# Hyena filters kept as sum and difference, their channel sums as columns, and one listed order for taps, norms, spectra and projections

## The chip, the core and the metric

The kernel runs on one core of a Trainium2 chip, as one launch. The metric is device time in microseconds (us); the median of 3 runs of the kernel before is 1652.36 us (1650.11 to 1653.74). The engines are named as the profile names them: PE is TensorE, PEld its weight loads, DVE is VectorE, ACT is ScalarE, POOL is GpSimd, and SP is the queue that issues the DMAs.

## The reference, cut to what matters

Two transformer blocks on a sequence of 512 rows and a context of 256 rows, 1024 wide. Block 0 mixes with an FFT over groups and with a long convolution (Hyena), block 1 with latent attention; a gated FFN follows each. The change lies in block 0, in the filters of the long convolution:

```
h = h @ w4                                # [L, 1024]: 512 forward, 512 backward taps
h_fwd = h[:, :D_HYENA] * decay
h_bwd = h[:, D_HYENA:] * decay
two_sided = concat([h_fwd, zeros(1), h_bwd[:0:-1]])
two_sided = two_sided / sum(abs(two_sided), axis=0)
spectrum = rfft(two_sided)                # for L = 512 and for L = 256
...
u_h = dwconv3(proj[..., D_FOURIER:], conv_w, conv_b)
x0, x1, v = split(u_h, 3)
y_h = x0 * long_conv(v * x1, spectrum, hy_bias)
```

## The kernel before, in words

All products are in three passes: an operand is split into a high part in fp32r (ACT, helper `hi`, lines 119 to 124) and a low remainder (DVE, helper `lo`, line 129), and `mm3` (lines 149 to 151) adds high by high, low by high and high by low. So a weight tile takes a DMA (`wr`), an ACT copy (`wh`), a DVE subtraction (`wl`) and then the matmuls. `wr`, `wh` and `wl` have three buffers each, and the large PSUM tiles `mm` (two banks each) three, the small ones `ms` two.

`mixer` first makes the filter MLP, the norm and three projections (m = 0, 1, 2) in an order written out by hand, up to the third sine of the MLP, `h3`. What follows is the stage of the change:

- There are six time tiles of 128 taps, two (4 and 5) for the context and four (0 to 3) for the sequence. `time_tile` makes one: `filter_mm` (line 421) two fp32 matmuls of 512 columns, forward and backward; `filter_pm` multiplies each by the decay on DVE (lines 430 and 431), then POOL adds and subtracts (line 437, twice), ACT makes the high parts `aph` and `amh`, takes the absolute values (lines 441 and 442), and POOL adds those (line 443); `filter_lo` makes the low parts on DVE.
- `filter_sum` sums the absolute values over the taps: one fp32 matmul of 512 columns for each tile against a 128 by 128 matrix of a constant (line 459), so that the sum stands in all 128 rows; then a reciprocal over 128 by 512 on DVE (line 461).
- `filter_spec` makes one spectrum tile: a cosine half and a sine half, 6 matmuls each for the context (two spectra) and 12 each for the sequence (four spectra). `filter_scale` multiplies by the reciprocal on DVE (lines 497 and 499) and adds the skip row on POOL (498). `filter_nyquist` (line 475) makes one further row.
- Between them stand projections 3, 4 and 5 (`proj`, `hconv`): 48 matmuls each, and for 4 and 5 a convolution over three taps, whose first step is on ACT (line 371) and the other two on DVE (lines 372 and 373), reading PSUM. After the stage come projections 12, 8, 13, 9 and so on, each with such a convolution; `fold` (POOL, line 696, then DVE, lines 701 and 702) and the transposes of `turn` on PE (line 708) stand between them.
- `gemv_dve` (line 241) computes modulation rows on DVE from a 512 KB weight tile; 14 of them are spread over this stage and the projections after it.

The stage before is written step by step, and the scheduler of the tile layer chooses the order on each engine, but for two waits on the last step of the norm (`issue_after`). An engine works through its queue in order.

Of the kernel before, what the change touches and what calls it, by code (L numbers as in the profile page):

```python
# [18 lines left out]
P = 128  # L19
# [45 lines left out]

MIX_ORDER = """
# [10 lines left out]
class Builder:  # L77
# [118 lines left out]
    def load_sb(self):  # L196
        nc = self.nc
        for j in range(2):
            nc.sync.dma_start(self.sb[:, j, :], self.I["cboth"][j : j + 1, :].partition_broadcast(P))
            nc.scalar.activation(self.sb[:, j, :], self.sb[:, j, :], AF.Silu)  # L200

# [31 lines left out]
    def gemv_dve(self, i, jt, conds=(0, 1)):  # L233

        nc = self.nc
        raw = self.t(self.W, [P, 1024], F32, "wr")
        nc.sync.dma_start(raw, self.I["wmodT"][i, jt])
        for j in conds:
            junk = self.t(self.sbp, [P, D], BF16, "junk", 1)
            acc = self.t(self.sm, [P, 1], F32, "gacc", 4)  # L240
            nc.vector.scalar_tensor_tensor(junk, raw, 1.0, self.sb[:, j, :], op0=ALU.mult, op1=ALU.mult, accum_out=acc)  # L241
            nc.vector.tensor_tensor(self.mod[i][:, jt, j : j + 1], acc, self.col(f"bm_{i}", jt), op=ALU.add)
# [174 lines left out]
    def filter_mm(self, h3, tt):  # L417
        ps = self.mm()
        r0, c = 64 * (tt // 3), 128 * (tt % 3)
        for q in range(2):  # L420
            self.nc.tensor.matmul(ps[:, 512 * q : 512 * q + 512], h3[r0 : r0 + 64, c : c + 128], self.w4[r0 : r0 + 64, 512 * q : 512 * q + 512],
                                  start=True, stop=True)
        return ps

    def filter_pm(self, ps, dec, first):

        nc, v = self.nc, self.nc.vector
        f = self.t(self.S2, [P, 512], F32, "s2")
        b = self.t(self.S2, [P, 512], F32, "s2")
        v.tensor_tensor(f, ps[:, 0:512], dec, op=ALU.mult)  # L430
        v.tensor_tensor(b, ps[:, 512:1024], dec, op=ALU.mult)
        if first:
            v.memset(b[0:1, :], 0.0)
        parts = []
        for tg, op in (("ap", ALU.add), ("am", ALU.subtract)):
            s = self.t(self.S2, [P, 512], F32, "s2")
            nc.gpsimd.tensor_tensor(s, f, b, op=op)  # L437
            hi = self.t(self.pg, [P, 512], F32R, tg + "h", 4)
            self.hi(hi, s)
            parts.append((s, hi))  # L440
        nc.scalar.activation(f, f, AF.Abs)
        nc.scalar.activation(b, b, AF.Abs)
        nc.gpsimd.tensor_tensor(f, f, b, op=ALU.add)
        return parts, f

    def filter_lo(self, parts):
        out = []
        for tg, (s, hi) in zip(("ap", "am"), parts):
            lo = self.t(self.pg, [P, 512], F32R, tg + "l", 4)
            self.lo(lo, s, hi)  # L450
            out.append((hi, lo))
        return out

    def filter_sum(self, sums, nhalf):

        ps = self.ms()
        on = self.onesN[nhalf]
        for i, f in enumerate(sums):
            self.nc.tensor.matmul(ps, on, f, start=i == 0, stop=i == len(sums) - 1)
        S = self.t(self.pf, [P, 512], F32, "S")  # L460
        self.nc.vector.reciprocal(S, ps)
        return S

    def filter_skip(self, nhalf):
        B = self.brow
        self.nc.vector.tensor_scalar(B, B, self.bscale / nhalf, None, op0=ALU.mult)
        self.bscale = nhalf

    def filter_nyquist(self, a, S):
        v = self.nc.vector  # L470
        ps = self.ms()
        nt = len(a)
        for i in range(nt):
            for q in range(2):
                self.nc.tensor.matmul(ps[0:1, :], self.altr, a[i][0][q], start=i == 0 and q == 0, stop=i == nt - 1 and q == 1)
        ny = self.t(self.S2, [P, 512], F32, "s2")
        v.tensor_tensor(ny[0:1, :], ps[0:1, :], S[0:1, :], op=ALU.mult)
        v.tensor_tensor(ny[0:1, :], ny[0:1, :], self.brow[0:1, :], op=ALU.add)
        return ny

    def filter_spec(self, a, tb):

        nt = len(a)
        th, tl = tb
        ps = self.mm()
        for c in range(2):
            for i in range(nt):
                w = slice(256 * i + 128 * c, 256 * i + 128 * c + 128)
                self.mm3(ps[:, 512 * c : 512 * c + 512], th[:, w], tl[:, w], a[i][c][0], a[i][c][1], i == 0, i == nt - 1)
        return ps  # L490

# [1357 lines left out]
```

## Time and profile before

| | |
|---|---|
| median of 3 runs | 1652.36 us |
| profiled execution, time | 1653.27 us |
| its span | 1651.5 us |
| PE, busy share of the span | 97% |
| DVE, busy share | 64% |
| ACT, busy share | 37% |
| POOL, busy share | 8% |
| granted PE clock, mean | 0.987 |

The span runs from the first to the last instruction of the profiled execution, and all times in the trace count from its start. The profile gives for each instruction its start, its duration and, where its engine stood idle before it, what ended the idle time. Ends of matmuls are modelled, so the rate of a run of matmuls is better read from the starts of the first and of the one that follows the last.

### The profile page before, as it was taken

Reading aid. Unit: us, or ns where it says so; the run is one execution under the profiler, and the core shown is the slowest. Engines: PE = TensorE matmul, PEld = TensorE weight load, DVE = VectorE, ACT = ScalarE, POOL = GpSimd, SP = SyncE. Lnnn points to the kernel's source line nnn. Section 1 sums busy time; section 2 is a strip of 40 time slices with the busy share of each in tenths; the row PEclk is TensorE's granted clock in tenths of the full one; section 3 lists DMA queues with packets and bytes.
Section 4 is the critical chain, followed back from the end, with each engine's and each line's share of the span. In section 5 each row is a group of like instructions: output and inputs, shape, how many; then the busy total and the mean of one; then the engine's idle time right before and its main releaser. Section 6 shows DMA issues by size and latency. Waiting matters only on the chain.

```text
span 1651.5 us, 20777 instructions
## 1 busy us (share of the span) xinstructions
PE 1598.3 (97%) x8228; PEld 1298.8 (79%) x8228; DVE 1057.5 (64%) x1696; ACT 616.9 (37%) x876; POOL 125.5 (8%) x177
## 2 busy tenths in 40 slices
PE   7989998999999999999998999999999999999999
PEld 5757887888888888888887887666659878878877
DVE  6788869977877354553443576899987544344243
ACT  4432224424222112322122245989864432233131
POOL 0151115000000000000000000222210000000000
PEclk9999999999999999999999999999999999999999
DMA  9325411532444134431430420000014222222222
GB/s 360 118 77 184 173 58 62 181 136 92 154 153 152 64 128 140 145 137 64 140 115 29 147 68 20 13 10 13 1 70 162 88 101 91 89 102 91 89 90 89
DMA packets 54541, 173.35 MB, mean 105 GB/s; under 512 B 6187, under 2 KB 9453, under 8 KB 53421
## 3 DMA queue, kind: packets, MB, share of 16 engines
q1 hardware_dynamic: 54445, 172.03, 29.8%
q8 instruction: 65, 1.06, 0.3%
q14 instruction: 31, 0.25, 0.1%
HBM read 166.24 MB, written 5.77 MB: 104 GB/s over the span
## 4 chain that ended last, share of the span: by engine, by line
PE 77%; DVE 14%; issue 2%; POOL 2%; ACT 2%; DMA 2%; POOLq 0%; SPq 0%; DVEq 0%; ACTq 0%
PE mm L149 23%; PE mm L151 22%; PE mm L150 22%; PE pv L1519 2%; DVE S L1495 1%; DVE wl L129 1%; PE s L1465 1%; DVE junk L241 1%; POOL s L437 1%; DVE wr L1534 1%; PE k L149 1%; PE k L151 1%; PE k L150 1%; DVE hl L311 1%; DMA wm<-wmod0a 1%
## 5 line engine op out<-in xcount | busy, mean ns | idle before, releaser
L149 PE MATMUL mm<-hh,wh 128*128 128x512 f32 (+2 forms) x1360 | 481.9, 357 | 8.4 <-DVE x L373 6.6
L150 PE MATMUL mm<-hl,wh 128*128 128x512 f32 (+2 forms) x1360 | 479.6, 353 | 2.3 <-DVE hl L311 2.3
L151 PE MATMUL mm<-hh,wl 128*128 128x512 f32 (+2 forms) x1360 | 479.3, 353 | 1.6 <-DVE wl L129 1.6
L124 ACT ACTIVATE wh<-wr 128x1024 fp32r<-128x1024 f32 (+2 forms) x192 | 197.6, 1032 | 583.4 <-PE mm L150 545.3
L129 DVE TENSOR_TENSOR wl<-wr,wh 128x1024 fp32r<-128x1024 f32 (+2 forms) x192 | 233.8, 1220 | 253.4 <-ACT wh L124 251.7
L149 PEld LDWEIGHTS mm<-hh,wh 128*128 128x128 f32 x1360 | 256.8, 189 | 56.5 <-issue 14.6
L150 PEld LDWEIGHTS mm<-hl,wh 128*128 128x128 f32 x1360 | 257.3, 189 | 40.4 <-DVE hl L311 3.5
L151 PEld LDWEIGHTS mm<-hh,wl 128*128 128x128 f32 x1360 | 257.1, 189 | 38.4 <-DVE wl L129 1.8
L241 DVE SCALAR_TENSOR_TENSOR junk<-wr,sb 128x1024 bf16<-128x1024 f32 x128 | 157.2, 1228 | 31.6 <-DMA wr<-wmodT 31.0
L151 PE MATMUL mm<-ah,wl 128*128 128x512 f32 (+1 forms) x480 | 172.4, 359 | 0.0
L150 PE MATMUL mm<-al,wh 128*128 128x512 f32 (+1 forms) x480 | 172.2, 359 | 0.0
L149 PE MATMUL mm<-ah,wh 128*128 128x512 f32 (+1 forms) x480 | 172.1, 359 | 0.0
L1061 DVE SCALAR_TENSOR_TENSOR xr<-mm,mod,xr 128x512 f32<-128x512 f32 (+1 forms) x100 | 61.8, 632 | 152.3 <-PE mm L151 150.6
L149 PEld LDWEIGHTS mm<-ah,wh 128*128 128x128 f32 x480 | 90.3, 188 | 14.8 <-issue 0.2
L150 PEld LDWEIGHTS mm<-al,wh 128*128 128x128 f32 x480 | 90.3, 188 | 14.6
L151 PEld LDWEIGHTS mm<-ah,wl 128*128 128x128 f32 x480 | 90.2, 188 | 14.5
L1519 PE MATMUL pv<-S,V 128*128 128x512 f32 x192 | 93.8, 597 | 2.7 <-ACT S L1498 2.7
L1085 ACT ACTIVATE fg<-fg 128x772 f32<-128x772 f32 (+1 forms) x44 | 32.6, 741 | 98.4 <-DVE fg L373 98.3
L1473 ACT ACTIVATE S<-s,rks 128x512 f32<-128x512 f32 x96 | 62.6, 685 | 12.2 <-PE pv L1519 8.3
L1519 PEld LDWEIGHTS pv<-S,V 128*128 128x128 f32 x192 | 34.4, 190 | 34.9 <-issue 29.4
L1491 POOL PARTITION_ALL_REDUCE mx<-mx x16 | 45.2, 2823 | 163.1 <-DVE mx L1488 163.1
L1495 DVE TENSOR_TENSOR S<-S,mx 128x1536 f32<-128x1536 f32 x32 | 55.3, 1749 | 2.3 <-POOL mx L1491 2.3
(333 smaller groups left out, 2290.1 us busy)
## 6 DMA issues: line engine op xcount, KB each, us to landing
wr<-w_up SPq DMA_DIRECT2D x88, 512.0 KB, 3.2
wr<-wmodT SPq DMA_DIRECT2D x80, 512.0 KB, 3.2
wr<-w_dn SPq DMA_DIRECT2D x32, 512.0 KB, 3.2
wm<-wmod0a SPq DMA_DIRECT2D x8, 1024.0 KB, 9.0
wr<-w_in SPq DMA_DIRECT2D x16, 512.0 KB, 3.3
wr<-w_out SPq DMA_DIRECT2D x13, 512.0 KB, 3.3
wr<-w_dn SPq DMA_DIRECT2D x17, 384.0 KB, 3.3
wr<-w_o SPq DMA_DIRECT2D x11, 512.0 KB, 3.2
```

The costliest lines, as they stand in the source:

```text
L124: self.nc.scalar.activation(dst, src, AF.Copy)
L129: (eng or self.nc.vector).tensor_tensor(dst, src, hi.bitcast(F32), op=ALU.subtract)
L149: mmul(out, wh, xh, start=start, stop=False)
L150: mmul(out, wh, xl, start=False, stop=False)
L151: mmul(out, wl, xh, start=False, stop=stop)
L241: nc.vector.scalar_tensor_tensor(junk, raw, 1.0, self.sb[:, j, :], op0=ALU.mult, op1=ALU.mult, accum_out=acc)
L1061: nc.vector.scalar_tensor_tensor(x[m][:, a2:b2], ps[:, a2:b2], mod[:, 8 * sec + m, c : c + 1], x[m][:, a2:b2], op0=ALU.mult, op1=ALU.add)
L1085: nc.scalar.activation(g[:, :n], g[:, :n], AF.Silu)
L1473: nc.scalar.activation(c.S[a][j // 3][:, j % 3, :], c.ps[a, j], AF.Copy, scale=c.r[:, g : g + 1])
L1491: nc.gpsimd.partition_all_reduce(c.m[a][:, 1, :], c.m[a][:, 0, :], P, bass.bass_isa.ReduceOp.max)
L1495: v.tensor_tensor(c.S[a][h], c.S[a][h], mb.to_broadcast([P, 3, T]), op=ALU.subtract)
L1519: nc.tensor.matmul(c.P[a], V[:, j, o : o + 128], c.S[a][j // 3][:, j % 3, :], start=j == 0, stop=j == 5)
```

## The change

What it does, part by part:

1. `filter_w4` replaces the forward and backward columns of the weight `w4` by their sum and their difference, before the taps are made: two POOL instructions and one ACT copy, placed inside the norm, after step 0 of row block 4. The tap matmuls then give sum and difference at once, so POOL's add and subtract for each time tile go away. Row 0 of tiles 0 and 4, where the backward tap is zero, is mended by one DVE and two ACT instructions on one row (`f_row`, `f_row2`).
2. |forward| + |backward| is taken as the greater of |sum| and |difference|: one DVE instruction for each tile (`f_max`) in place of POOL's addition. The tiles are then added on POOL (`f_add`, one instruction for the context, three for the sequence).
3. The sum over the taps has the data as the stationary operand and a column of the constant as the moving one (`f_sum`, four matmuls of 1 column), so that the sums stand as 4 columns; the reciprocal is of 128 by 4 (`f_rec`); four matmuls against the identity spread it over the rows (`f_spread`), and ACT copies it (`f_scale`).
4. The whole stage, from the first tap to the last half spectrum, with projections 3, 4 and 5, the loads for projection 12 and six of the 14 `gemv_dve`, is a list of steps, `FILTER_ORDER`, and the order of PE, DVE, ACT and POOL is that of the list. The DMAs stand in the order that the scheduler gives them. Each half of a spectrum and each quarter of a projection is a step of its own.
5. Eight `gemv_dve` stay in the loop over projections 12, 8, 13 and so on, in the counts 0, 1, 1, 2, 1, 2, 1 (before: 1, 2, 1, 2, 1, 2, 2, after three in the stage).
6. The loads of the skip row and of the modulation input are issued before the stage; the Silu on the latter becomes a step of the list.

Lines in the kernel after are 9 higher than before in the helpers: `hi` is line 133, `lo` 138, and `mm3` 158 to 160.

```diff
+FILTER_ORDER = """
+D0 MM0 PMa0 MM5 Rb R4 PMb0 U0 R3 PMb5 PMa5 MM4 D3 PMb4 WH3 U2 PMa4 WH4 U1 WL3 RR0 D1 WHb SB RR4 MM2 Z0 MM3 SK1
...
-    def filter_pm(self, ps, dec, first):
...
-        v.tensor_tensor(f, ps[:, 0:512], dec, op=ALU.mult)
-        v.tensor_tensor(b, ps[:, 512:1024], dec, op=ALU.mult)
...
-            nc.gpsimd.tensor_tensor(s, f, b, op=op)
...
-        nc.scalar.activation(f, f, AF.Abs)
-        nc.scalar.activation(b, b, AF.Abs)
-        nc.gpsimd.tensor_tensor(f, f, b, op=ALU.add)
...
+    def filter_w4(self):
+
+        f, b = self.w4[:, 0:512], self.w4[:, 512:1024]
+        t = self.t(self.S2, [P, 512], F32, "s2")
+        self.nc.gpsimd.tensor_tensor(t, f, b, op=ALU.add)
+        self.nc.gpsimd.tensor_tensor(b, f, b, op=ALU.subtract)
+        self.nc.scalar.copy(f, t)
...
-            self.onesN[nh] = self.t(self.pf, [P, P], F32, f"on{int(nh)}")
+            self.onesN[nh] = self.t(self.pf, [P, 1], F32, f"on{int(nh)}")
...
+                if d == 4:
+                    self.filter_w4()
...
+        def f_taps(t):
+            ps = q_["m" + t] = self.mm()
+            r0, c = 64 * (int(t) // 3), 128 * (int(t) % 3)
+            for q in range(2):
+                w = slice(512 * q, 512 * q + 512)
+                nc.tensor.matmul(ps[:, w], h3[r0 : r0 + 64, c : c + 128], self.w4[r0 : r0 + 64, w], start=True, stop=True)
+
+        def f_mul(c, t):
+            q_[f"s{c}" + t] = tp()
+            v.tensor_tensor(q_[f"s{c}" + t], q_["m" + t][:, 512 * c : 512 * c + 512], dec[int(t)], op=ALU.mult)
...
+        def f_max(t):
+
+            q_["f" + t] = tp()
+            v.tensor_tensor(q_["f" + t], q_["s0" + t], q_["s1" + t], op=ALU.max)
+
+        def f_add(n):
+            a, b = {"c": "45", "01": "01", "23": "23", "x": "02"}[n]
+            nc.gpsimd.tensor_tensor(q_["f" + a], q_["f" + a], q_["f" + b], op=ALU.add)
+
+        def f_sum(s_):
+            rt, f = self.ms(), q_["f4" if s_ == "c" else "f0"]
+            for b in range(4):
+                nc.tensor.matmul(rt[:, b : b + 1], f[:, P * b : P * b + P], self.onesN[256.0 if s_ == "c" else 512.0], start=True, stop=True)
...
+        def f_spread(s_):
+            R = q_["sp" + s_] = self.ms()
+            for b in range(4):
+                nc.tensor.matmul(R[:, P * b : P * b + P], q_["rc" + s_][:, b : b + 1].to_broadcast([P, P]), self.ident, start=True, stop=True)
...
-            hconv(12 + i, cv, 1 if i < 3 else 2)
+            hconv(12 + i, cv, (0, 1, 1, 2, 1, 2, 1)[2 * i], None if i else q_["w6"])
...
-                hconv(8 + i, cx, 2)
+                hconv(8 + i, cx, (0, 1, 1, 2, 1, 2, 1)[2 * i + 1])
```

How the instructions move, at three places. The first is ACT's queue around the first step of projection 4's convolution, which reads PSUM tile `mm_927` before and `mm_926` after and writes `x_16`; `aph` and `amh` (before), `a0h` and `a1h` (after) are the high parts of sum and difference of a time tile, the rows that write an `s` tile over itself are absolute values, and `wh` is the high part of a weight or table. Before:

```order
L124 ACTIVATE amh_890<-s_199_888 128x512
L441 ACTIVATE s_195_879<-s_195_879 128x512
L442 ACTIVATE s_196_880<-s_196_880 128x512
L124 ACTIVATE aph_908<-s_206_906 128x512
L124 ACTIVATE amh_912<-s_208_910 128x512
L441 ACTIVATE s_204_902<-s_204_902 128x512
L442 ACTIVATE s_205_903<-s_205_903 128x512
L371 ACTIVATE x_16_109<-mm_927,pcol_67 128x772
L124 ACTIVATE wh_1169<-wr_1167 128x1024
```

And after, the same step of the convolution (line 724 now):

```order
L644 ACTIVATE s_210_913<-s_210_913 128x512
L644 ACTIVATE s_203_877<-s_203_877 128x512
L644 ACTIVATE s_199_857<-s_199_857 128x512
L644 ACTIVATE s_196_816<-s_196_816 128x512
L133 ACTIVATE wh_1094<-wr_1019 128x1024
L724 ACTIVATE x_16_109<-mm_926,pcol_67 128x772
L644 ACTIVATE s_178_768<-s_178_768 128x512
L644 ACTIVATE s_181_777<-s_181_777 128x512
L133 ACTIVATE wh_1119<-wr_1100 128x1024
```

Before, the step stood behind the high parts of time tile 1, whose sources `s_206` and `s_208` POOL writes. After, all sources of ACT in front of it are written by DVE or loaded, and four absolute values and one table stand ahead of it.

The second is PE's queue from the end of projection 5 (`mm_1039`) to the first spectrum of the sequence (`mm_1125`), with the sums over the taps (`ms_1111`). Before:

```order
L151 MATMUL mm_1039<-hh_114_373,wl_1036 128x260
L459 MATMUL ms_1111<-s_204_902,on_13_103 128x512
L459 MATMUL ms_1111<-s_222_992,on_13_103 128x512
L459 MATMUL ms_1111<-s_231_1014,on_13_103 128x512
L149 MATMUL mm_1125<-aph_886,wh_1121 128x512
```

After, the sums of the sequence stand between two half spectra, the second half of `mm_1122` and the second half of `mm_1106`:

```order
L158 MATMUL mm_1122<-a1h_981,wh_1094 128x512
L159 MATMUL mm_1122<-a1l_982,wh_1094 128x512
L160 MATMUL mm_1122<-a1h_981,wl_1095 128x512
L658 MATMUL ms_1168<-on_13_103,s_242_1073 128x1 x4
L158 MATMUL mm_1106<-a1h_812,wh_923 128x512
```

The sums left the front of the spectra: before, all spectra of the sequence stood behind them in PE's queue; after, three half spectra stand ahead of them.

The third is DVE's queue from the reciprocal of the context's sums to the scaled spectra. `junk` is half a `gemv_dve`, `wl` the low part of a weight or table, and `S` the spread reciprocal. Before:

```order
L461 RECIPROCAL S_822<-ms_819 128x512
L129 TENSOR_TENSOR wl_1036<-wr_1033,wh_1035 128x1024
L497 TENSOR_TENSOR s_187_845<-mm_832,S_822 128x512
L499 TENSOR_TENSOR s_188_846<-mm_832,S_822 128x512
L497 TENSOR_TENSOR s_190_863<-mm_850,S_822 128x512
```

After:

```order
L663 RECIPROCAL fsum_921<-ms_908 128x4
L243 SCALAR_TENSOR_TENSOR junk_960,gacc_961<-wr_944,sb_87 128x1024
L244 TENSOR_TENSOR mod_4_73<-gacc_961,pcol_67 128x1
L243 SCALAR_TENSOR_TENSOR junk_964,gacc_965<-wr_944,sb_87 128x1024
L244 TENSOR_TENSOR mod_4_73<-gacc_965,pcol_67 128x1
L695 TENSOR_TENSOR s_227_975<-mm_867,S_958 128x512
L695 TENSOR_TENSOR s_228_977<-mm_867,S_958 128x512
```

Between the reciprocal and its use there now stand a whole `gemv_dve` on DVE and, on PE and ACT, the spread and its copy.

More of the change, by code (lines that the diff above doesn't have):

```diff
@@ L446, in filter_lo @@
[L446 to L479, printed above, removed]
@@ L671, in mixer @@
[L671 to L686 removed]
+        Hs = {}
@@ new lines, in f_mul, with f_row, f_row2 @@
+        def f_mul(c, t):
+            q_[f"s{c}" + t] = tp()
+            v.tensor_tensor(q_[f"s{c}" + t], q_["m" + t][:, 512 * c : 512 * c + 512], dec[int(t)], op=ALU.mult)
+        def f_row(t):
+            q_["row" + t] = tp()
+            v.tensor_tensor(q_["row" + t][0:1, :], q_["s0" + t][0:1, :], q_["s1" + t][0:1, :], op=ALU.add)
+        def f_row2(t):
+            for c in range(2):
+                nc.scalar.activation(q_[f"s{c}" + t][0:1, :], q_["row" + t][0:1, :], AF.Copy, scale=0.5)
@@ new lines, in f_part, with f_skip_add, f_keep, f_ny @@
+        def f_part(c, n):
+            q_[f"h{c}" + n] = tp()
+            v.tensor_tensor(q_[f"h{c}" + n], q_["p" + n][:, 512 * c : 512 * c + 512], q_["S" + n[0]], op=ALU.mult)
+        def f_skip_add(n):
+            nc.gpsimd.tensor_tensor(q_["h0" + n], q_["h0" + n], self.brow, op=ALU.add)
+        def f_keep(c, n):
+            nc.sync.dma_start(Hd[key(n)][c], q_[f"h{c}" + n])
+        def f_ny(s_):
+            ps = q_["ny" + s_] = self.ms()
+            ts = tiles[s_]
+            for i, t in enumerate(ts):
+                for q in range(2):
+                    nc.tensor.matmul(ps[0:1, :], self.altr, ah[t][0][q], start=i == 0 and q == 0, stop=i == len(ts) - 1 and q == 1)
@@ new lines, in f_step @@
+        def f_step(s_):
+            if s_ == "SB":
+                f_silu()
+            elif s_ == "U3":
+                nc.scalar.copy(Uf[3], q_["q3"][:, :TW])
+            elif s_[0] == "U":
+                nc.scalar.copy(Uf[int(s_[1])], ps3[int(s_[1])][:, :TW])
+            else:
+                k = max((k for k in steps if s_.startswith(k)), key=len)
+                steps[k](s_[len(k) :])
+        with self.tc.manual_schedule(engines={ENG.PE, ENG.DVE, ENG.Activation, ENG.Pool}):
+            for s_ in FILTER_ORDER.split():
+                f_step(s_)
@@ L687, in mixer @@
+        for n in ("c0", "c1", "x0"):
+            Hs[key(n)] = [q_["h0" + n], q_["h1" + n]]
+        nyc, ny = q_["nc"], q_["nx"]
         self.close("pg")
```

183 lines of the change are left out of this document (100 added, 83 removed).

## The prediction

> **What bounds the kernel now.** I read the page first, then a table of stretches around the filters, then PE's waits there, then the timelines of PE, POOL, ACT and DVE at the longest wait.
>
> ```profile
> span 1651.5 us, 20777 instructions
> PE 1598.3 (97%) x8228; PEld 1298.8 (79%) x8228; DVE 1057.5 (64%) x1696; ACT 616.9 (37%) x876; POOL 125.5 (8%) x177
> ```
>
> PE is the bound: 53 us of the span are not PE's. So a change that takes no matmuls away can gain only PE's idle time and time at a lower clock. The stretches cover the stage; the columns are the stretch, its length, then busy time and instructions of PE, PEld, DVE, ACT and POOL, the granted clock, and the DMA's share and rate:
>
> ```profile
> 107.00:115.00 8.00, 1.41 (x5) 0.42 (x3) 7.42 (x12) 4.13 (x6) 4.54 (x3) 0.75 0.19 67
> 115.00:129.00 14.00, 12.07 (x53) 9.33 (x54) 9.32 (x11) 6.42 (x10) 9.47 (x6) 0.90 0.22 75
> 129.00:154.00 25.00, 25.00 (x107) 19.05 (x106) 22.84 (x31) 3.36 (x5) 3.87 (x3) 1.00 0.47 162
> 154.00:179.00 25.00, 25.00 (x143) 21.84 (x142) 20.98 (x37) 4.80 (x5) 2.11 (x2) 1.00 0.74 259
> 179.00:190.00 11.00, 9.05 (x46) 7.68 (x45) 9.78 (x21) 2.75 (x3) 1.99 (x2) 0.84 0.39 132
> ```
>
> PE loses 6.6 us in 107:115, and around that wait the granted clock falls to 0.75 and 0.90. PE's waits from 70 to 205 us, with total, times and longest:
>
> ```profile
> PE mm L149 <- DVE x L373: 6.6, 1, 6.6
> PE ms L459 <- POOL s L443: 3.2, 3, 1.9
> PE mm L708 <- ACT tm L371: 1.9, 1, 1.9
> PE mm L708 <- DVE tm L701: 0.6, 1, 0.6
> ```
>
> The first is projection 5 waiting for a PSUM tile that projection 4's convolution still reads. Who made DVE late stands in the timelines of POOL, ACT and DVE:
>
> ```profile
> 105.87 3.73 POOL L437 TENSOR_TENSOR s<-s,s 128x512 f32<-128x512 f32 x2
> 108.22 0.63 ACT L124 ACTIVATE aph<-s 128x512 fp32r<-128x512 f32 x1 [3.67 <-POOL s L437]
> 111.20 0.97 ACT L371 ACTIVATE x<-mm,pcol 128x772 f32<-128x772 f32 x1
> 113.75 1.01 DVE L373 SCALAR_TENSOR_TENSOR x<-mm,pcol,x 128x771 f32<-128x771 f32 x1
> ```
>
> Projection 4's first convolution step stood in ACT's queue behind the high part of a time tile, and that waited for POOL. The three waits at L459 (the sums) are POOL's too. So 9.8 us (6.6 + 3.2) hang on POOL's part in the taps, which the change removes.
>
> **The prices.** PE, from starts in its timeline:
>
> ```profile
> 14.20 1.05 PE L278 MATMUL ms<-ones,s 128*128 128x1 f32 x8 [1.17 <-DVE s L272]
> 20.79 1.05 PE L296 MATMUL ms<-cst,rq_r 128*128 128x128 f32 x8
> 70.68 3.70 PE L421 MATMUL mm<-w,s 64*128 64x512 f32 x8
> 74.31 0.50 PE L149 MATMUL mm<-hh,wh 128*128 128x512 f32 x1
> 85.97 0.79 PE L149 MATMUL mm<-aph,wh 128*128 128x512 f32 x1
> 91.99 0.40 PE L475 MATMUL ms<-aph,altr 128*1 128x512 f32 x1
> 97.79 0.39 PE L149 MATMUL mm<-hh,wh 128*128 128x512 f32 x1
> 104.12 0.39 PE L149 MATMUL mm<-hh,wh 128*128 128x512 f32 x1
> 114.90 0.77 PE L149 MATMUL mm<-hh,wh 128*128 128x512 f32 x1 [6.59 <-DVE x L373]
> 124.78 1.88 PE L459 MATMUL ms<-s,on 128*128 128x512 f32 x4
> 135.16 0.40 PE L475 MATMUL ms<-aph,altr 128*1 128x512 f32 x1
> 137.02 0.39 PE L149 MATMUL mm<-aph,wh 128*128 128x512 f32 x1
> 142.64 0.40 PE L149 MATMUL mm<-aph,wh 128*128 128x512 f32 x1
> ```
>
> - A time tile's taps: (74.31 - 70.68)/2 = 1.81 us. A projection: six of its eight parts take 104.12 - 97.79 = 6.33, so 8.44 in all. The context's two spectra: 91.99 - 85.97 = 6.02. One spectrum of the sequence: 142.64 - 137.02 = 5.62, a half 2.81. The Nyquist row of the sequence: 137.02 - 135.16 = 1.86, of the context half of it.
> - An old sum takes 1.88/2 = 0.94 (each instruction has two records), six take 5.6. The new sums in columns have the shape of the norm's L278, the spread that of L296: four instructions 1.05 each. Twice both is 4.2, so this edit is worth 1.4 on PE.
>
> DVE, POOL and ACT, from the groups between 70 and 154 us:
>
> ```profile
> L437 POOL TENSOR_TENSOR s<-s,s 128x512 f32<-128x512 f32 x12 | 20.0, 1693 | 79.4 <-DVE s L433 77.2 <-DVE mod L242 2.2
> L129 DVE TENSOR_TENSOR apl<-s,aph 128x512 fp32r<-128x512 f32 x6 | 7.4, 1234 | 5.8 <-ACT aph L124 5.8
> L461 DVE RECIPROCAL S<-ms 128x512 f32<-128x512 f32 x2 | 6.7, 3346 | 0.0
> L430 DVE TENSOR_TENSOR s<-mm,s 128x512 f32<-128x512 f32 x6 | 4.0, 668 | 0.0
> L241 DVE SCALAR_TENSOR_TENSOR junk<-wr,sb 128x1024 bf16<-128x1024 f32 x12 | 15.6, 1303 | 0.0
> L129 DVE TENSOR_TENSOR wl<-wr,wh 128x1024 fp32r<-128x1024 f32 (+1 forms) x11 | 15.0, 1367 | 4.3 <-ACT wh L124 4.3
> L441 ACT ACTIVATE s<-s 128x512 f32<-128x512 f32 x6 | 3.7, 614 | 0.0
> ```
>
> On DVE two reciprocals (6.7 us) go, six maxima (six times 0.67, the price of a multiplication of the same size) and two instructions on one row come: even, within 2 us. ACT gets two copies for the spread and four one-row instructions, six times 0.6 at most, and is busy less than half of each stretch but 107:115. On POOL twelve additions of 1.7 us go.
>
> Three more prices, with the two events that the sum is held against: ACT's takeover of projection 12's weight buffer, and the first transposes after the stage. The last row is of the page's DMA issues: size and time to landing of a weight of `gemv_dve`.
>
> ```profile
> 162.43 1.07 ACT L124 ACTIVATE wh<-wr 128x1024 fp32r<-128x1024 f32 x1 [7.52 <-PE mm L150]
> 175.98 1.01 DVE L372 SCALAR_TENSOR_TENSOR tm<-mm,pcol,tm 128x771 f32<-128x771 f32 x1
> 178.18 2.13 POOL L696 TENSOR_TENSOR tm<-tm,tm 128x512 f32<-128x512 f32 x1 [21.76 <-issue]
> 181.42 0.98 PE L708 MATMUL mm<-cst,tm 128*128 128x128 f32 x6 [1.95 <-ACT tm L371]
> wr<-wmodT SPq DMA_DIRECT2D x80, 512.0 KB, 3.2
> ```
>
> **The sum, walked forward.** The old list and the new part at PE's first tap, 70.7 us; before it only `filter_w4` is new. Its POOL pair can run as soon as the weight lands, its ACT copy stands in the norm between the high parts of row blocks 4 and 5. I cost it at nothing, since PE's start at 70.7 is set by the row blocks after it, and say 1 us if the copy delays block 5 in full (0.6) and POOL slows DVE. From 70.7, PE does, in the order of the list:
>
> - five taps, 9.1, to 79.8; projection 3, 8.4, to 88.2; the last tap, 1.8, to 90.0
> - the context's four half spectra, 6.0, to 96.0; its sums, 1.05, to 97.1
> - projection 4 with spread and Nyquist row inside, 8.4 + 1.05 + 0.9, to 107.5; projection 5 to 115.9
> - three half spectra, 8.4, to 124.3; sums to 125.4; a half to 128.2; spread and Nyquist to 131.1
> - two halves, 5.6, to 136.7; projection 12 with the last two halves inside (the scheduler put them there), 8.4 + 5.6, to 150.8.
>
> Against that I held the other queues, with 0.6 us for a 512-wide step of ACT or DVE, 1.0 for `wh` and 1.2 for `wl` (the mean of 1.37 stands partly beside POOL's additions), 2.6 for a `gemv_dve`. Seven places can make PE wait:
>
> 1. Taps 2 and 3 reuse PSUM tiles that DVE empties in two products each. The first tap ends at 72.5, its products at 73.8; wanted at 76.1.
> 2. Projection 3 needs its `wl`, on DVE behind the third tap's products: 76.1 + 1.3 + 1.2 = 78.6; wanted at 79.8.
> 3. One context table's `wh` reuses the buffer of projection 3's weight. ACT makes it after 88.2, DVE its half-sized `wl` by 89.5; wanted at 91.5, after the first half spectrum.
> 4. The context's sums need POOL's one addition, behind a product, a maximum, two low parts and a maximum on DVE: 90.0 + 5 times 0.6 + 1.7 = 94.7; wanted at 96.0.
> 5. Projection 5 reuses the PSUM tile of a context spectrum. The spread stands behind a quarter of projection 4, done at 100.2; copy 0.6, two products 1.3: 102.1; wanted at 107.5. The `gemv_dve` ahead of the products runs meanwhile.
> 6. The sequence's first half spectrum needs the last low part. From 102.1 DVE has the Nyquist row (ready at 103, two steps), two `wl` and six low parts, to 110.3; wanted at 115.9. The convolution of projection 4 has only to be done by 118.7.
> 7. Closest are two behind the second spread. Table 2's `wh` reuses the buffer freed at 128.2: `wl` done at 130.4, wanted at 131.1. And the last half ahead of projection 12 needs a PSUM tile emptied behind a `gemv_dve`, whose weight takes the buffer that table 0's `wl` frees near 127.7: landed at 130.9, done at 133.5, tile free at 134.1, wanted at 133.9. I count 0.5.
>
> So projection 12 ends near 151.3. Before, that was at 162.4 (the first of the rows above).
>
> The gain to that point is 162.4 - 151.3 = 11.1 us. Taken the other way: 9.8 of waits, 1.4 of sums, and the slow clock after the long wait (0.90 in 115:129, 14 times 0.10 = 1.4) make 12.6, less the 0.5. I take 11.0, the lower.
>
> Next come the first transposes. They waited 1.95 us: projection 8's convolution stood behind `gemv_dve` on DVE until 175.98, then POOL from 178.18, then DVE's fold, 3.2 from POOL's start to the transposes. The clock then was 0.84 in 179:190, 11 times 0.16 = 1.8 us more. Now three `gemv_dve` (7.8 us of DVE) fewer stand in this loop. From 134.1 DVE's queue holds, up to the end of that convolution, three `gemv_dve` (7.8), the Nyquist row (1.3) and four products (2.4) of the list, then eight halves of `gemv_dve` (10.4), three `wl` (3.6), a product (0.6) and four convolution steps (4.0): 164.2, and 3.2 more gives 167.4. PE comes at 151.3 + 16.9 = 168.2: a tie within my error of a microsecond or two. Of the 3.7 us I take half, 1.8.
>
> On the clock the Trainium skill ("TensorE: Matmul & The Clock Gate", HAM oscillation — how this bites in real kernels) has a rule: no idle gaps of over about 3.4 us, for those drop PE to half rate. The row disagrees here: 1.95 us of idle was followed by 0.84. By the rule the wait at the transposes would cost 1.95 alone, and the sum would be 0.9 smaller.
>
> Sum: 11.0 + 1.8 = 12.8 us. The profiled execution took 1653.3, so it would take 1640.5; the median lay 0.9 below it, so I say **1639.6**.
>
> **The rivals.**
>
> - *The close places miss.* Places 4 and 7 have 1.3, 0.7 and -0.2 us to spare, from rows with errors of that size. If each misses by 1.5 and one slow clock of 1.8 follows, 4.5 + 1.8 = 6.3 are lost: 1645.9. For it speaks that a low part beside POOL takes 1234 ns on average, where a product of the same size takes 668; against it, that POOL has little left to do.
> - *More goes.* The transposes' wait goes whole with its clock, and the second one (0.6): 11.0 + 3.7 + 0.6 = 15.3, or 1637.1; with the two ways of counting apart by 1.6, down to 1635.5.
> - *No change.* PE comes earlier to the mixing stage, and DVE is what that waits for. DVE is busy 20.98 of 25 us in 154:179. But it has three `gemv_dve` less there and the same count in all by then. If DVE kept its old times, nearly all would be given back: 1651.
> - *Slower: the clock stays low.* PE is handed from one PSUM tile to the next with waits of a few tenths, from 70 to 151 us, and the clock counts them. At half clock all along, the 80.6 us from 70.7 to 151.3 would take 80.6 more; a quarter of that is 20, so 20 - 11 = 9 slower, 1661. It decides from the point where more than 11/80.6, a seventh, of the stretch is at half clock. Against it: the longest wait of the sums, 1.9 us, left 1.00 in 129:154, so short waits alone do not do it. The same page of the Trainium skill (A second HAM failure mode: psum-queue depth-cycling) tells of kernels where just such handing over does; no run shown so far has it.
>
> **How the numbers follow.** This measurement can tell about 0.2%, 3.3 us, from no change. The forecast, a gain of 9 to 15 us, has 0.62; the close places 0.18; more 0.08; no change 0.05; slower 0.07. The range takes in the forecast and most of the first two rivals: 1635.5 (all of the second) to 1647 (the first, and 1 us for `filter_w4`). Faster: 0.62 + 0.18 + 0.08 = 0.88; the same 0.05; slower 0.07.
>
> **What would show it.** Right: no wait of PE on POOL's taps and none at projection 5; projection 12 done within 150 to 154 us; granted clock 1.00 from 72 to 150; the first transpose near 168 to 170 with under 1 us of wait; from there the old trace, shifted. Wrong: PE's first tap later than 71.5 (`filter_w4`); waits over 1 us at sums, half spectra or projection 5; a clock under 0.95 in the stage; or the shift lost again between 170 and 300.

## The result, and the profile after

The changed kernel takes **1642.62 us** in the median of four runs (1639.44 to 1645.42), the kernel before 1651.74 (four runs, 1650.11 to 1653.74): a ratio of 0.9944 with a 95% interval of 0.9922 to 0.9965. The gain is about 9 us in the medians; the two profiled executions differ by 13.8 us (1639.44 to 1653.27). The page, and then the table of stretches with the columns of the prediction:

```profile
span 1637.7 us, 20805 instructions
...
PE 1588.3 (97%) x8248; PEld 1297.1 (79%) x8248; DVE 1047.6 (64%) x1702; ACT 621.0 (38%) x883; POOL 109.6 (7%) x165
```

```profile
107.00:115.00 8.00, 8.00 (x43) 6.83 (x43) 7.93 (x13) 5.34 (x7) 2.15 (x1) 1.00 0.21 73
115.00:129.00 14.00, 14.00 (x69) 10.84 (x69) 9.66 (x15) 2.71 (x3) 5.73 (x4) 1.00 0.43 140
129.00:154.00 25.00, 22.04 (x109) 17.79 (x108) 24.66 (x44) 3.59 (x4) 6.70 (x4) 1.00 0.64 213
154.00:179.00 25.00, 24.93 (x144) 21.64 (x143) 23.61 (x45) 6.57 (x8) 2.92 (x2) 1.00 0.66 222
179.00:190.00 11.00, 9.02 (x53) 7.70 (x52) 9.81 (x20) 3.15 (x4) 2.88 (x2) 1.00 0.51 174
```

PE is busy without a gap from 107 to 129, at a granted clock of 1.00, where it had lost 6.6 us and run at 0.75 and 0.90. What it loses now lies behind 129 and in 179:190. All of PE's waits from 60 to 205 us:

```profile
PE mm L158 <- DVE s L695: 3.0, 3, 2.1
PE mm L787 <- DVE tm L780: 2.0, 1, 2.0
```

The waits on POOL and the one at projection 5 are gone; those at L695 (a product with the reciprocal, which frees a PSUM tile) are new, and the one at L787 is the second transposes. PE at the first tap, at the new sums and spread, at the longest wait and at the two transposes, from its timeline:

```profile
69.60 6.54 PE L616 MATMUL mm<-w,s 64*128 64x512 f32 x20
76.07 0.50 PE L158 MATMUL mm<-hh,wh 128*128 128x512 f32 x1
...
120.69 0.95 PE L658 MATMUL ms<-on,s 128*128 128x1 f32 x8
121.50 0.47 PE L158 MATMUL mm<-a1h,wh 128*128 128x512 f32 x1
...
124.39 1.05 PE L668 MATMUL ms<-cst,fsum 128*128 128x128 f32 x8
125.20 0.47 PE L708 MATMUL ms<-a0h,altr 128*1 128x512 f32 x1
...
132.16 0.50 PE L158 MATMUL mm<-a0h,wh 128*128 128x512 f32 x1 [2.05 <-DVE s L695]
...
167.67 0.98 PE L787 MATMUL mm<-cst,tm 128*128 128x128 f32 x6
187.49 0.97 PE L787 MATMUL mm<-cst,tm 128*128 128x128 f32 x6 [1.98 <-DVE tm L780]
```

Before, the first transposes began at 181.42 and the second, from the same view of the kernel before, at 201.45:

```profile
201.45 0.79 PE L708 MATMUL mm<-cst,tm 128*128 128x128 f32 x5 [0.64 <-DVE tm L701]
```

So PE is 1.1 us ahead of the old kernel at the first tap (70.68 to 69.60), 13.8 at the first transposes and 14.0 at the second. That would be the end of it if the rest of the program ran as before. It does not. The same matmuls matched by name in both traces show PE's lead growing from 14.0 at 400 us to 15.3 at 880, falling from 14.7 at 980 to 9.5 at 1010, and growing again to 13.8 at the end. No edit touches any of that code. (Matched by name means: each matmul is paired with the one that has the same operands and the same place in the sequence, and the lead is the difference of their starts.)

### The profile page after: what moved, and what is told of

Read it like the earlier page. It is cut to its first block, busy times and chain, and to the rows that moved or that the text cites. A ratio compares the mean times of both kernels' runs of the same rounds, so it can differ in the third digit from the quotient of the medians.

```text
span 1637.7 us, 20805 instructions
## 1 busy us (share of the span) xinstructions
PE 1588.3 (97%) x8248; PEld 1297.1 (79%) x8248; DVE 1047.6 (64%) x1702; ACT 621.0 (38%) x883; POOL 109.6 (7%) x165
## 4 chain that ended last, share of the span: by engine, by line
PE 79%; DVE 15%; issue 2%; ACT 2%; DMA 1%; POOL 1%; SPq 0%; POOLq 0%; ACTq 0%; DVEq 0%
PE mm L158 23%; PE mm L160 23%; PE mm L159 23%; PE pv L1598 2%; DVE junk L243 2%; DVE wl L138 1%; DVE S L1574 1%; PE s L1544 1%; DVE wr L1613 1%; PE k L158 1%; PE k L160 1%; PE k L159 1%; DVE hl L313 1%; PE mm L616 1%; DVE mx L1558 0%
## 5 line engine op out<-in xcount | busy, mean ns | idle before, releaser
L133 ACT ACTIVATE wh<-wr 128x1024 fp32r<-128x1024 f32 (+1 forms) x192 | 197.8, 1033 | 564.7 <-PE mm L159 527.3
```

What stands on the lines that cost most here:

```text
L133: self.nc.scalar.activation(dst, src, AF.Copy)
```

## The experiments

**Theory P**, the prediction's: POOL's part in the taps caused the 9.8 us of waits and their slow clock; the list only places the steps. **Rival L**: the order caused them. The first four kernels undo or do one part each; the others were made when the first traces showed the two effects behind 400 us.

In these runs the kernel before had medians of 1651.2 to 1653.8; each ratio is to its runs on the same chip. The table has the median, the ratio to the kernel before with its interval, PE's lead over the kernel before at the end of the filters (150 us) and behind the second transposes (190), both less what it was at the first tap, the change of the lead between 980 and 1010, and the matmuls that PE does in 1500 to 1600 us.

| kernel | us | ratio | 150 | 190 | 980 to 1010 | matmuls |
|---|---|---|---|---|---|---|
| before | | 1 | 0 | 0 | 0 | 430 |
| after | 1642.62 | 0.9944 [0.9922, 0.9965] | 10.7 | 12.9 | -5.2 | 435 |
| a_taps_only | 1646.32 | 0.9961 [0.9945, 0.9978] | 9.1 | 8.5 | -0.4 | 430 |
| b_taps_and_columns | 1643.42 | 0.9956 [0.9941, 0.9970] | 5.6 | 6.9 | -0.2 | 436 |
| d_list_with_pool_taps | 1645.89 | 0.9964 [0.9951, 0.9977] | 6.7 | 7.5 | -6.9 | 436 |
| e_list_with_row_sums | 1653.31 | 1.0001 [0.9990, 1.0012] | 6.4 | 7.2 | -8.4 | 430 |
| f_before_shifted | 1649.83 | 0.9971 [0.9959, 0.9983] | 0.0 | 0.5 | -0.2 | 435 |
| g_after_unshifted | 1646.14 | 0.9953 [0.9936, 0.9970] | 11.0 | 11.9 | -4.3 | 430 |
| h_g2_later | 1640.63 | 0.9920 [0.9901, 0.9940] | 12.1 | 15.2 | -7.0 | 436 |
| i_psum_turned | 1630.85 | 0.9863 [0.9847, 0.9879] | 12.1 | 15.8 | +0.7 | 435 |
| j_two_gemv_later | 1632.91 | 0.9874 [0.9857, 0.9890] | 12.3 | 14.1 | +0.7 | 435 |
| k_shift64 | 1636.97, one run | | 12.3 | 14.5 | +2.1 | 430 |
| l_shift32 | 1637.37, one run | | 12.4 | 14.7 | -0.4 | 429 |
| m_stage_alone | 1640.44 | 0.9930 [0.9913, 0.9948] | 11.0 | 11.7 | +1.8 | 430 |

### a: the taps' edit alone

```diff
 def filter_pm(self, ps, dec, first):
...
         if first:
-            v.memset(b[0:1, :], 0.0)
...
-            s = self.t(self.S2, [P, 512], F32, "s2")
-            nc.gpsimd.tensor_tensor(s, f, b, op=op)
...
-        nc.gpsimd.tensor_tensor(f, f, b, op=ALU.add)
...
+        self.nc.vector.tensor_tensor(m, f, b, op=ALU.max)
...
+                if d == 4:
+                    self.filter_w4()
```

> The kernel before, in the scheduler's own order and with its six sums by rows, but with the filters' weight replaced by sum and difference ahead of the taps, so that POOL's twelve additions and subtractions go, and with the maximum on DVE in place of POOL's six sums of magnitudes. Theory P (POOL's part in the taps causes the 9.8 us of waits): the 6.6 us at projection 5 and the 3.2 us at the sums are under 1 us each, the slow clock behind them goes, 9.8 to 11.2 us off: 1640.5 to 1642. Rival L (the order causes them: projection 4's convolution stays in ACT's queue behind a high part, whoever makes that late): a wait of 3 us or more at projection 5 stays, 0 to 5 us off: 1647 to 1652.

Measured 1646.32. PE's waits from 60 to 160 us are two of 0.2 us:

```profile
PE ms L474 <- DVE s L458: 0.2, 1, 0.2
PE mm L429 <- DVE s L514: 0.2, 1, 0.2
```

At 150 us PE leads by 9.1 us. Without POOL's pairs the waits go, as theory P says. But the scheduler also chose a new order. Projection 4's first convolution step (L371) now stands ahead of the high part of time tile 1; before, it stood behind that (111.20, behind 108.22):

```profile
106.35 0.98 ACT L371 ACTIVATE x<-mm,pcol 128x772 f32<-128x772 f32 x1
107.23 0.61 ACT L124 ACTIVATE aph<-s 128x512 fp32r<-128x512 f32 x1
```

So this run alone does not tell POOL's lateness from the step's place in ACT's queue; run d tries the other half. The time was 4 us over the theory's range: the first transposes wait as before (a 2.6 us wait on DVE's L719, clock 0.93 in 154:179), and only 6.4 us of the expected 9.8 or more reach the end.

### b: all arithmetic, no list

```diff
 def filter_sum(self, sums, nhalf):
-        for i, f in enumerate(sums):
-            self.nc.tensor.matmul(ps, on, f, start=i == 0, stop=i == len(sums) - 1)
...
+        while len(sums) > 1:
+            for i in range(len(sums) // 2):
+                nc.gpsimd.tensor_tensor(sums[2 * i], sums[2 * i], sums[2 * i + 1], op=ALU.add)
+            sums = sums[::2]
...
+            nc.tensor.matmul(rt[:, b : b + 1], sums[0][:, P * b : P * b + P], self.onesN[nhalf], start=True, stop=True)
...
-        self.nc.vector.reciprocal(S, ps)
```

> The same, and the sums as columns with their spread as in the changed kernel; all arithmetic of the change, none of its list. Theory P: the sums are worth 1.4 us more, 1639 to 1640.5, so as fast as the changed kernel or faster. Rival L: without the list the sums bring four new hand-overs (POOL's additions, sum, reciprocal, spread, copy) that PE waits for with nothing put between, at 1 to 2 us for each of the two sums, and the time is 2 us or more above the changed kernel's, 1645 to 1652.

Measured 1643.42, 0.8 over the changed kernel, so neither range for the time holds. In the stage L is right: the sums wait for the new hand-overs.

```profile
PE ms L478 <- POOL s L474: 4.1, 2, 2.1
...
PE mm L149 <- DVE x L373: 1.8, 1, 1.8
```

The lead at 150 is 5.6 in place of 9.1. Without a list, column sums cost the stage 3.5 us; the list takes that away. Yet the total is the changed kernel's. So the list must lose elsewhere what it gains here (the column 980 to 1010), and the columns must gain somewhere (the last column).

### d: the list, with POOL's pairs put back

```diff
+            f, b = q_["s0" + t], q_["s1" + t]
+            q_["s0" + t] = tp()
+            nc.gpsimd.tensor_tensor(q_["s0" + t], f, b, op=ALU.add)
+            nc.gpsimd.tensor_tensor(b, f, b, op=ALU.subtract)
...
-                if d == 4:
-                    self.filter_w4()
```

> The changed kernel with its list, but the weight stays as it was and POOL makes the sum and the difference of each time tile again (twelve operations, each pair put right behind its two products in the list). The maximum stays on DVE. Theory P: POOL's 20 us come back into the chain; the last pair can end no earlier than 20.4 us after the first products (73.8), 94.2, or later where POOL waits, and high parts and sums behind it hold PE at the context's sums, at projection 5 or at the first half spectrum of the sequence, 5 us or more in all: 1648 or more. Rival L: the list has projections between, POOL's pairs are hidden behind them, PE waits under 2 us more in 70 to 155: 1642.5 to 1645.

Measured 1645.89, between the two. PE's waits in 60 to 160 us are 6.1 in all, 3.1 more than in the changed kernel:

```profile
PE mm L158 <- DVE s L694: 2.9, 3, 2.1
PE mm L160 <- DVE wl L138: 1.5, 1, 1.5
PE mm L158 <- DVE s L618: 1.3, 1, 1.3
PE ms L657 <- POOL s L652: 0.4, 1, 0.4
```

The list hides most of POOL's 20 us but not all. The wait of 6.6 us at projection 5 is not among these rows, though POOL makes all its pairs again. So the list's order alone removes it, with POOL as late as before. A kernel without POOL's pairs in the old order was not run, since in a the scheduler moved the step too. This run also answers for `filter_w4`: without it PE's first tap is at the same time to 0.05 us, so it costs nothing at that point.

### e: the list, with row sums

```diff
 def f_sum(s_):
+            for i, t in enumerate(ts):
+                nc.tensor.matmul(rt, self.onesN[256.0 if s_ == "c" else 512.0], q_["f" + t], start=i == 0, stop=i == len(ts) - 1)
...
 def f_rec(s_):
+            v.reciprocal(q_["S" + s_], q_["rt" + s_])
```

> The changed kernel with its list, but the sums by rows as before: two and four fp32 matmuls of 512 columns, reciprocals of 128x512 on DVE, no spread, no copy, no additions on POOL. By the prediction's prices PE has 5.6 us in place of 4.2, so 1.4 more, and DVE 6.7 us more at the two sums, of which 0 to 2 reach PE at the second one (table 2 and the tile behind the gemv_dve): 1644 to 1646. Rival: PE's price of the sums is hidden (other waits become shorter by as much), or POOL's additions and the copies that go make up for it: 1641.5 to 1643.

Measured 1653.31: both theories are wrong by 7 us and more. At 150 us 4.3 us of the lead are gone, some of them as expected (the wait on L692 is 3.2, one of 0.9 on a `wl`, and a slow clock of 0.93 in 129:154). The rest is lost behind 400 us, in code that is the same.

### f and g: the place of the tiles in SBUF

The six kernels so far fall into two groups: with row sums PE does 430 matmuls in 1500 to 1600 us, with column sums 435 or 436. The column sums add 10 matmuls to PE's program ahead of that, and two small tiles of 24 columns to a pool that stays open: 2 times 24 times 4 bytes lift all tiles of later pools by 192 bytes in each partition. One kernel adds these tiles, unused, to the kernel before; the other moves them to a pool that closes with the filters.

```diff
 # f, on the kernel before
+        for _ in range(2):
+            v.memset(self.t(self.sm, [P, 24], F32, "fsum"), 1.0)
 # g, on the changed kernel
-            q_["rc" + s_] = self.t(self.sm, [P, 24], F32, "fsum")
+            q_["rc" + s_] = self.t(self.pf, [P, 24], F32, "fsum")
```

> The kernel before, with one thing added: the two small tiles (128x24, 192 bytes in each partition) that the changed kernel keeps in the pool of small tiles for its column sums are allocated there and set once by DVE, and not used. All tiles of later pools then lie 192 bytes higher, as in the changed kernel; instructions of PE are the same as before. In the five traces so far the later blocks (400 to 880 and 1010 to 1630 us), which no edit touches, run 5.6 us faster in the three kernels with column sums than in the three with row sums. Theory A (the address of the tiles decides): this kernel gets that 5.6 us, 1646 to 1648, and PE's pace in the later blocks is that of the changed kernel. Rival I (the place of the instructions in PE's program decides, which has 10 matmuls more with column sums): later blocks as before, 1651 to 1653.

> The changed kernel, with these two small tiles in a pool that is closed after the filters, so that the tiles of later pools lie where they lay before; PE's instructions are those of the changed kernel. Theory A: the later blocks lose 5.6 us, 1647 to 1649, and what is left of the gain is the filter stage's, 4 to 5 us. Rival I: no change in the later blocks, 1641.5 to 1643.5.

Measured 1649.83 and 1646.14. The stretch 1500 to 1600 us with PE's busy time and matmuls, clock and DMA, of the kernel before, the changed kernel, f and g:

```profile
1500.00:1600.00 100.00, 100.00 (x430) 1.00 0.27 92
```

```profile
1500.00:1600.00 100.00, 100.00 (x435) 1.00 0.27 90
```

```profile
1500.00:1600.00 100.00, 100.00 (x435) 1.00 0.29 92
```

```profile
1500.00:1600.00 100.00, 100.00 (x430) 1.00 0.27 89
```

PE is busy all the time at full clock in all four, and still 1.2% apart; the pace goes with the place of the tiles and not with the 10 matmuls. Theory A is shown by the pace. From 400 to 880 and from 1300 to 1640 us the lead of f grows by 1.4 and 3.3 us, as that of the changed kernel does (1.3 and 3.3); that of g grows by 0.0 and 0.1. So f shows 4.7 of the 5.6 us; from 1010 to 1300 it loses 1.8, with a clock of 0.97 in 1200:1300. In the medians f gains 4.8 us (0.9971, interval 2.8 to 6.8 us), clear of noise. g's loss is not: its ratio is 0.9953, the changed kernel's 0.9944, some 1.5 us between them, and the intervals overlap. g came out 0.9 us better than expected, f 1.8 worse.

### h: one gemv_dve behind the product

```diff
-... SDAx3 RG2 G2 SQx3 SDBx3 NYx SDAx1 RG3 G0 ...
+... SDAx3 RG2 SQx3 SDBx3 G2 NYx SDAx1 RG3 G0 ...
```

> The changed kernel with one entry of the list moved: the gemv_dve ahead of the product that PE waits 2.05 us for at 130.1 (half spectrum ahead of projection 12) stands behind that product. Theory (the prediction's place 7: the gemv_dve on DVE holds the PSUM tile): that wait falls under 0.5 us, 1.5 to 2.0 us off, 1640.5 to 1641.5, if the second transposes do not take it back. Rival (DVE is the bound from there on, and its queue is as long as before): PE waits as much more at the transposes, 1642 to 1643.

Measured 1640.63, inside the theory's range. The wait of 2.05 us is gone and the one at the second transposes fell from 2.0 to 0.6; a later one at L695 grew to 1.3. PE's lead at 190 us is 2.3 us more. In the medians that is 2.0 us, which the two intervals cannot separate.

### i: the place in PSUM

Between 980 and 1010 us the kernels with the list (the changed one, d, e, g, h) have a wait of 3.4 to 3.7 us, and those without it (the kernel before, a, b, f) have none over 0.3 us. Of the changed kernel, PE's and DVE's timeline there:

```profile
984.31 1.50 PE L1319 MATMUL ms<-cst,rq_r 128*128 128x128 f32 x12
...
989.52 0.50 PE L158 MATMUL k<-wh,qah 128*128 128x192 f32 x1 [3.71 <-DVE pt L1326]
```

```profile
987.31 1.01 DVE L1419 SCALAR_TENSOR_TENSOR kp<-mm,pcol,ropeK 64x772 f32<-64x772 f32 x1 [2.91 <-ACT sqpe L1417]
988.25 1.12 DVE L1326 SCALAR_TENSOR_TENSOR pt<-mm,pcol,pt 128x512 f32<-128x512 f32 x2
```

Of the kernel before:

```profile
999.00 1.50 PE L1240 MATMUL ms<-cst,rq_r 128*128 128x128 f32 x12
1000.26 0.33 PE L149 MATMUL k<-wh,qah 128*128 128x192 f32 x1
```

After the matmuls at L1319 the old kernel goes straight on to the queries' product; the new one waits 3.71 us until DVE has read a tile `mm` at L1326. There the pool of the three PSUM tiles `mm` closes and another opens over it. The explanation, which the next kernel tests since no view shows addresses: in the changed program the tile that DVE still reads lies under the new pool's first tile, in the old program elsewhere; the list changed the order in which tiles come free in block 0, and everything after takes its turn from there. In 985:1003 the granted clock is 0.72, against 0.81 in 999:1017 of the kernel before, 18 times 0.09 = 1.6 us more; with the wait that is 5.3, and the lead falls by 5.2. One unused tile turns the places back:

```diff
+            skip = self.mm()
+            v.memset(skip[:, 0:1], 0.0)
             pqa = self.mm()
```

> The kernel h_g2_later with one thing added: one PSUM tile of the pool of three is allocated and set in one column by DVE ahead of the query projections of block 1 and not used, so that the tiles after it take the places that they have in the kernel before. In the traces of the five kernels with the list PE waits 3.7 to 4.0 us in block 1 near 986 us (the first tile of the next PSUM pool lies over the tile that DVE's L1326 reads), in the four without it PE does not. Theory B (the list changed the order in which PSUM tiles come free, and so the places): that wait goes, 3.7 us, with the slow clock behind it up to 5.2 us: 1635.4 to 1637. Rival: DVE or ACT is late there for another reason (their queues since 900 us), the wait stays or another of the same size takes its place: 1640 to 1641.

Measured 1630.85: theory B, and 4.6 us under its range. PE's waits from 960 to 1010 us:

```profile
PE k L158 <- ACT K L133: 0.5, 1, 0.5
PE pv L158 <- ACT V L1591: 0.5, 1, 0.5
```

Against h the lead over this stretch is 7.7 us better, since h had lost 7.0 there and not 5.2; the medians are 9.8 apart, and the 2.1 us between stay open. This kernel beats both: 22.7 us under the kernel before (0.9863, 20.0 to 25.3).

### j: two more gemv_dve moved

```diff
-KAx3 G3 KBx3 SDAx2 RG4 SQx2 G4 SDAx0 SPBx2 ...
+KAx3 KBx3 SDAx2 G3 RG4 SQx2 SDAx0 G4 SPBx2 ...
```

> i_psum_turned with two more entries of the list moved: the gemv_dve G3 behind the product that frees the tile waited for at 140.8 (1.3 us), G4 behind the one at 145.1 (0.6 us). Theory (these are again the prediction's place 7, a gemv_dve ahead of a product): both waits under 0.3 us, 1.5 to 1.9 us off i_psum_turned. Rival (DVE's queue is the bound: it is busy from 125 to 152 without a gap of 0.3 us): the gemv_dve come back as a wait at the first or second transposes, within 0.5 us of i_psum_turned.

Measured 1632.91. The theory fell: the two waits at L695 stayed (1.21 and 0.46 us), since the product waited for still stands behind the gemv_dve G0 and the Nyquist row, and the transposes wait 2.3 us where they waited 0.6. As the rival said, what is moved comes back. But the median is 2.1 us over i_psum_turned, where the rival allowed 0.5; the two intervals overlap, so whether the move costs anything stays open.

### k and l: other distances

```diff
+        v.memset(self.t(self.sm, [P, 16], F32, "pad", 1), 1.0)   # k
+        v.memset(self.t(self.sm, [P, 8], F32, "pad", 1), 1.0)    # l
```

> j_two_gemv_later with 64 bytes more in each partition in the pool of small tiles, so that tiles of later pools lie 64 bytes higher. In the kernels so far the fast place of these tiles is an odd multiple of 64 bytes, the slow one an even multiple (192 bytes apart), while the weights lie at multiples of 256. Theory A64 (the place modulo 128 decides): later blocks at the slow pace, 5 to 6 us more than j_two_gemv_later between 400 and the end. Rival (it is not the distance modulo 128): the fast pace stays, within 1 us.

> The same with 32 bytes in place of 64. Theory A64 with a step of 64 bytes (what lies in the same half of 128 bytes is the same place): fast pace, within 1 us of j_two_gemv_later. Rival (the step is finer, 32 bytes): another pace, faster or slower by over 1 us between 400 and the end.

The stretch 1500 to 1600 us in k (256 bytes above the kernel before) and l (224 bytes):

```profile
1500.00:1600.00 100.00, 100.00 (x430) 1.00 0.27 89
```

```profile
1500.00:1600.00 100.00, 100.00 (x429) 1.00 0.26 89
```

Both are slow here. k keeps the pace of the kernel before, as A64 says: its lead over that kernel changes by under 0.1 us from 400 to 880 and from 1300 to 1640 us. l has a pattern of its own (its lead grows by 0.6 us in the first of these stretches and shrinks by 1.0 in the second), so the step is finer than 64 bytes. Of the four places tried (0, 192, 224, 256 bytes) only the one at 192 is fast; k and l ran once each, and these readings rest on their traces.

### m: the stage alone

```diff
-            q_["rc" + s_] = self.t(self.sm, [P, 24], F32, "fsum")
+            q_["rc" + s_] = self.t(self.pf, [P, 24], F32, "fsum")
...
+            skip = self.mm()
+            v.memset(skip[:, 0:1], 0.0)
             pqa = self.mm()
```

> The changed kernel without its two side effects: the two small tiles lie in the pool that is closed after the filters (g_after_unshifted), and one unused PSUM tile is taken ahead of block 1's query projections (i_psum_turned), so that SBUF and PSUM places of block 1's later tiles are those of the kernel before. What is left of the gain is the filter stage's and the transposes'. In the traces that is 12.9 us (13.95 between the two kernels at 190 us, less 1.08 at the first tap); the prediction's sum was 12.8. Theory (the predicted gain is whole there, and the two side effects, 5.6 us gained and 5.2 us lost, nearly cancel): 12 to 14 us under the kernel before, 1639.5 to 1641.5, and no wait near 986 us. Rival (the medians' 9 to 10 us are the stage's true worth, and the profiled execution flattered it): 1643 to 1645.

Measured 1640.44, a ratio of 0.9930 (0.9913 to 0.9948) to 1651.23, that is 11.6 us (8.6 to 14.4). The time lies in the theory's range, but the gain is 0.4 us under its 12 to 14, because the range was counted from 1653.5 and the kernel before ran at 1651.2 here; the rival's 9 us lies near the interval's end and is not excluded. In the trace the wait near 986 us is gone. The second transposes wait 2.0 us as in the changed kernel, but here the clock falls behind it (0.92 in 190:210, 20 times 0.08 = 1.6 us), so the lead is 11.7 in place of 12.9.

## Why the prediction was right, and where it was not

- **The cause.** PE's waits on POOL went. Run a shows that the taps' edit removes them without the list, d that the list removes the longest of them without that edit; so of the two things that the prediction named, POOL's lateness and the step's place behind it in ACT's queue, changing the place was enough for that wait. What POOL's pairs alone are worth in the old order is not shown. Two of the prices held: a low part that had taken 1234 ns beside POOL takes 674, a product 680, as these groups of 70.7 to 154 us say.

```profile
L695 DVE TENSOR_TENSOR s<-mm,S 128x512 f32<-128x512 f32 x12 | 7.8, 680 | 0.9 <-ACT S L672 0.9
...
L138 DVE TENSOR_TENSOR a1l<-s,a1h 128x512 fp32r<-128x512 f32 x6 | 4.0, 674 | 0.0
```

- **First tap and `filter_w4`.** 69.60 in place of 70.7. The 1.1 us are clock at the start (0.98 in 0:69 before, 1.00 now), which is luck and not the change; `filter_w4` costs nothing, by d.
- **The taps.** Counted 1.81 us each, so 9.1 for five; the first five take 76.07 - 69.60 = 6.47. The price came from tiles 4 and 5, which use the same half of PE's 128 rows. Tiles 0 to 2 use one half, 3 to 5 the other, and the list takes 0, 5, 4, 2, 3; the trace shows matmuls of two tiles at once. The kernel before has that too, with tiles 2 and 3, whose matmuls start 0.01 us apart and take 1.93 us together:

```profile
105.26 1.99 PE L421 MATMUL mm<-w,s 64*128 64x512 f32 x8
107.19 1.13 PE L459 MATMUL ms<-s,on 128*128 128x512 f32 x2
```

In all the six taps take 6.47 + 1.91 = 8.4 us, before 3.63 + 3.62 + 1.93 = 9.2: 0.8 of the gain, which the prediction did not count.
- **The sums.** Counted 1.05 us for each four instructions, from the length of a row; from start to start they take 0.81 (121.50 - 120.69, 125.20 - 124.39). By starts an old sum takes 0.86 and not 0.94 (the first two begin at 124.78 and 125.64). So this edit is worth 5.2 - 3.3 = 1.9 on PE and not 1.4.
- **Places 1 to 6** do not wait. **Place 7** was named rightly and sized wrongly: 2.05 us, where 0.5 was counted; two more waits of the same kind (0.45 and 0.46) stand inside projection 12, where none was counted, 3.0 us in all. DVE freed the tile at 132.1 (the walk, moved by the 1.1 us of the first tap: 133.0), but PE wanted it at 130.1 and not at 132.8; PE did the steps ahead of it faster than the walk, above all the taps (2.6 us), so the wait grew and the end of projection 12, which DVE sets, moved little. Projection 12's first convolution step starts at 150.79; the walk said 151.3 - 1.1 = 150.2. The lead at 150 is 10.7; 11.0 was counted. With the measured terms the other way of counting closes: 9.8 of waits, 1.4 of clock, 1.9 of sums and 0.8 of taps, less 3.0, are 10.9.
- **The transposes.** The first lost their wait whole (3.7, not half); the second wait 2.0 in place of 0.6. Together the lead grew by 2.2 to 12.9; 1.8 was counted, 12.8 in all. That the clock stayed at 1.00 behind the second wait (190:210) is luck: in d, e, g and m waits of 1.9 to 2.0 us at the same place are followed by 0.91 or 0.92 in that stretch, some 1.6 to 1.8 us.
- **What failed** is the line "from there the old trace, shifted". Later tiles lie 192 bytes higher, which is worth 5.6 us (1.3 from 400 to 880, 4.3 from 1010 to the end; f shows 4.7 of it), and PSUM tiles take other places, which costs 5.2 at 986 us. The two nearly cancel, so that the sum met the end of the trace is luck; what the prediction reasoned about is the stage. There it was right to 0.3 us at projection 12 and 0.1 at the second transposes, and that too by terms that cancel: 2.5 us more of waits, against 0.8 of taps, 0.5 of sums and the 1.1 that it left out when it took the lower of its two ways.
- **Profile and median.** The profiled execution came to 1639.4, against 1640.5 forecast; but the median is 3.2 above it, where the prediction took 0.9 below. The changed kernel's four runs spread over 6 us, their mean granted clock from 0.985 to 0.990; the profiled one is the fastest of them and has the highest clock. So the sums of this section explain its 13.8 us and not the 9 of the medians, whose interval is 5.8 to 12.9 us.
- **The rivals.** The close places missed by 3.0 us in three waits, without a slow clock behind them. DVE did not give the gain back in the mixing stage, and the clock stayed at 1.00 from 107 to 190, so neither "no change" nor "slower" happened.

## What to carry to other kernels

When a change adds a tile or changes the order in which tiles come free, compare the traces to the very end, also where the code is the same: here unchanged code gained and lost some 40% of the gain (5.6 and 5.2 of 13.8 us). Match the same instructions in both traces and plot the lead; a step in it is a wait, a slope is a pace. And test an edit without its side effects on places before its worth is believed.

## What the runs showed of the hardware

- **Pace by SBUF place.** The same matmuls on the same shapes, PE busy 100% at clock 1.00, run 1.2% faster in 1500 to 1600 us with tiles at +192 bytes than at +0, +224 or +256. Why is open. The Trainium skill ("SBUF — State Buffer", Operand start alignment) lets an operand start at any multiple of its element size and says that its rule is about legality, not speed; no run here contradicts it, and by f the speed depends on the place.
- **Clock.** In the changed kernel two waits of 2.05 and 1.98 us left the clock at 1.00; the one of 3.71 us is followed by 0.72 in 985:1003. The Trainium skill's rule ("TensorE: Matmul & The Clock Gate", HAM oscillation — how this bites in real kernels) of no gap over about 3.4 us agrees with all three. It does not cover others: before, 1.95 us of idle was followed by 0.84, and in d, e, g and m waits of 1.88 to 1.98 us at the second transposes by 0.91 or 0.92 in 190:210. Nor is all of the 0.72 the wait's: the kernel before has 0.81 in 999:1017, where PE is busy 17.93 of 18 us.
- **A tiny DVE instruction beside POOL.** In the gemv_dve ahead of place 7, DVE's L244 on one column takes 1.13 us while POOL's addition runs, and 0.16 otherwise; the two rows of DVE, then POOL's:

```profile
129.04 1.13 DVE L244 TENSOR_TENSOR mod<-gacc,pcol 128x1 f32<-128x1 f32 x1
...
131.34 0.16 DVE L244 TENSOR_TENSOR mod<-gacc,pcol 128x1 f32<-128x1 f32 x1
```

```profile
128.01 2.14 POOL L698 TENSOR_TENSOR s<-s,brow 128x512 f32<-128x512 f32 x1 [6.69 <-DVE s L695]
```

L244 starts at 129.04 and ends at 130.17, just when the addition does (130.15): the instruction's size did not matter, the time left of POOL's did.
